# Decay scores as column tiles and dense norms in three parts, in a two-block transformer kernel

## The chip, the cores and the metric

The kernel runs on one core of a Trainium2 chip. The metric is the device time in microseconds (us) from the first to the last instruction of one execution and the little that lies around it; the median over several executions counts.

## What is computed

The reference takes 512 tokens of width 1024 through two blocks, all in float32. The first block has two layers, each with modulated RMS norm, sliding-window attention beside a pooling mixer, and a gated feed-forward part (width 2816). The second has a token mixer of two branches and a mixture of 32 experts. The change touches the norms between the parts of the first block and the first branch of the mixer, HGRN2 with 8 heads in both directions:

```python
x = x + gate_m * rms_norm(mix, g_post_mix[l])
h = rms_norm(x, g_pre_ffn[l]) * (1.0 + scale_f) + shift_f
f = (jax.nn.silu(h @ w_gate[l]) * (h @ w_up[l])) @ w_down[l]
x = x + gate_f * rms_norm(f, g_post_ffn[l])
...
# one direction of HGRN2: S_t = diag(f_t) S_{t-1} + k_t^T v_t, o_t = q_t S_t, k_t = 1 - f_t
decay = jnp.exp(jnp.where(causal, G[:, :, :, None, :] - G[:, :, None, :, :], -jnp.inf))
attn = jnp.einsum('bhtd,bhsd,bhtsd->bhts', qb, kb, decay)
o = jnp.einsum('bhts,bhsv->bhtv', attn, vb) + jnp.einsum('bhtd,bhdv->bhtv', qb * jnp.exp(G), S)
```

So the score of tokens s and t carries, for each of a head's 128 channels, the product of all forget gates f between them.

## The kernel before

**Layout and precision.** Activations lie transposed, channels on partitions and 512 tokens along a row, in eight blocks of 128 channels. Weights and activations are split into a high and a low part (`split_into`, L115: ACT writes the high part, DVE subtracts for the low one), and a product is three matmuls (`mm3`, L154: high by high, high by low, low by high). Weight slabs come by DMA on SP's queue into three `raw` buffers and are split into four `w` buffers (`W1`, L879), one for each 128 output columns. PSUM has four buffers `acc`, three `t` and one `mod`.

**The order of the work.** A planner fixes each engine's order when the kernel is built: of the instructions whose inputs and buffers it reckons ready, the one that stands earliest in the program goes next. On the chip each engine keeps that order and waits where an input is late. Moving a piece of code later therefore lowers its rank; it doesn't move it if nothing else is ready.

**Dense norms.** `out_phase` (L852) computes an output projection in eight blocks m; `slabs[m // 2]` holds the weights. In the last pass (`final`) blocks 0 to 3 are done for 512 tokens, then blocks 4 to 7 for the first 256 tokens and again for the last 256 (`half`). `stats` (L399) sums squares into `acc`. After block 7 of each half, `norms` (L420) is written out: `row_sums` (L344, PE, tile `st`), `rstd` (ACT's square root, DVE's reciprocal), `spread` (L355, PE, tile `rb`), and then for each of eight blocks the update of x and the next H, mostly on DVE. The next projection begins with the first half's tokens (`pj` in L706 for layer 1, `pg` and `pu` at L826 for the feed-forward part), with k in the outer loop over four weight tiles, and the first KE = 3 k steps of the second half after that. There are four such places with `final`: after the mixer and after the feed-forward part of each layer. After the fourth come the decay heads, whose first projection (`pj`) takes 512 tokens at once.

**Decay heads.** `hgrn` (L1155) projects, for each head, q, the two forget gates, the value (every second head) and the output gate. The rest of a head, `hg_head` (L1074), is a generator; `pump` (L449) lets it go one step for every 2.25 units of three matmuls of the next head, so its work stands between the next head's projections. KS holds the keys of both directions (1 - f), QP the queries times decay, TOT the products of f over growing runs of tokens. The scores between tokens of the same pair of runs, of h = 1, 2, 4, ... 64 tokens, are one level each: four matmuls of 128x128 (L1114, float32, two records each in the trace), of which only the entries of that level are wanted; `copy_predicated` (L1118) copies those by a mask into AD. Then `update` (L1084) multiplies KS on DVE (L1086) and QP on POOL (L1088) by the totals (tile `tot`, L1094), and `copies` (L1078) writes X and Y for the next level on ACT. Z (L1098, POOL) gives the scores of a token with itself (L1105). The products across 128-token chunks are `l1` (L1124) and `l2` (L1135). Last, the scores are split (`th` on ACT, `tl` on DVE, L1147 and L1148) and multiplied by the value (tile `po`), and `head_norm` (L1013) normalises the head with one reciprocal of 128x512 (L1026). The retention heads call it too.

Of the kernel before, what the change touches and what calls it, by code (L numbers as in the profile page):

```python
# [10 lines left out]
F32 = mybir.dt.float32  # L11
# [17 lines left out]
KE = 3  # L29
WG = 0  # L30
# [40 lines left out]
class K:  # L71
# [348 lines left out]
    def norms(self, h, F, gg, gs, sh, H):  # L420
# [4 lines left out]
        sums = self.row_sums(self.acc if both else self.acc[:1], h)  # L425
        r = self.small([128, 4], "rs", bufs=4)
# [250 lines left out]
    def layer(self, l, P, v, H, nxt, W=None):  # L677
# [138 lines left out]
        for nk in (6, 8, 8):  # L816
            G = []
            for j in range(k0 // 2, (k0 + nk) // 2):
# [9 lines left out]
                if j == 0:  # L828
                    for h, n in ((0, 8), (1, KE)):
                        for k in range(n):  # L830
                            for b in range(2):
                                self.gemm_cols(Wg, H, 8, b, pgu[b][0], half=h, ks=[k])
                                self.gemm_cols(Wu, H, 8, b, pgu[b][1], half=h, ks=[k])
# [18 lines left out]
    def out_phase(self, slabs, G, nk, F, final, gg, gs=None, sh=None):  # L852

        nc = self.nc
        newF = F or [self.blk("Q", F32, "f") for _ in range(8)]
        order = [(m, None) for m in range(4 if final else 8)]
        if final:
            order += [(m, h) for h in range(2) for m in range(4, 8)]
        pst = {}
        H = None  # L860
        for m, h in order:
            if m not in pst:
                pst[m] = self.ps("po")
            p = pst[m]
            self.gemm_cols(slabs[m // 2], G, nk, m % 2, p, half=h)
            hs = slice(0, 512) if h is None else slice(h * 256, h * 256 + 256)
            if F is None:
                nc.scalar.activation(newF[m][:, hs], p[:, hs], AF.Copy)
            else:
                nc.vector.tensor_tensor(newF[m][:, hs], newF[m][:, hs], p[:, hs], op=OP.add)  # L870
            if final:
                self.stats(newF[m][:, hs], m, hs, gg, gs is not None)
                if m == 7:
                    H = H or self.newH()
                    self.norms(h, newF, gg, gs, sh, H)
        return H or newF

# [14 lines left out]
    def block1(self):  # L892
# [21 lines left out]
        return self.layer(1, P1, v1, H, (None, None))  # L914
# [5 lines left out]
LEVELS = (1, 2, 4, 8, 16, 32, 64)  # L920
# [3 lines left out]
def const_masks():  # L924
    s = np.arange(128)[:, None]
    t = np.arange(128)[None, :]
    m = [(s // (2 * h) == t // (2 * h)) & (s // h != t // h) for h in LEVELS]
# [21 lines left out]
class K2(K):  # L949
    B2 = dict(O=16, M=8)  # L950
    HG = dict(KS=2, QP=2, X=2, Y=2, TA=1, TB=2, TH=2, TL=2, AD=1, q=2, T=2, sg=2)
# [61 lines left out]
    def head_norm(self, po, sg, g, n, O):  # L1013
# [12 lines left out]
        nc.vector.reciprocal(r, r)  # L1026
# [47 lines left out]
    def hg_head(self, j, KS, QP, TOT, q, V, sg, gcol, O):  # L1074
# [9 lines left out]
        def update(h, TOT):  # L1084
# [3 lines left out]
            nc.gpsimd.tensor_tensor(w, w, self.other(TOT, h, seg=1), op=OP.mult)  # L1088
# [7 lines left out]

        Z = self.blk("X", F32, "X")
        nc.gpsimd.tensor_tensor(Z, KS[:, 0:512], KS[:, 512:1024], op=OP.add)  # L1098
# [3 lines left out]
        p = self.ps("lv", tag="t")  # L1102
        for i in range(4):
            c = slice(i * 128, (i + 1) * 128)
            nc.tensor.matmul(p[:, c], lhsT=Z[:, c], rhs=q[:, c], start=True, stop=True)  # L1105
        AD = self.blk("AD", F32, "AD")
        nc.scalar.activation(AD, p, AF.Copy)
        yield
        ADv = AD.rearrange("p (i c) -> p i c", i=4)
        for li, h in enumerate(LEVELS):  # L1110
            p = self.ps("lv", tag="t")
            for i in range(4):
                c = slice(i * 128, (i + 1) * 128)
# [27 lines left out]
        for i in range(4):  # L1141
            th, tl = self.blk("TH", F32R, "th"), self.blk("TL", F32R, "tl")
            a = i // 2
            for dst, src in ((slice(i * 128, (i + 1) * 128), AD[:, i * 128:(i + 1) * 128]),
# [3 lines left out]
                nc.vector.tensor_tensor(tl[:, dst], src, th[:, dst].bitcast(F32), op=OP.subtract)  # L1148
            yield
            vs = slice(i % 2 * 256 + vc.start, i % 2 * 256 + vc.stop)  # L1150
            self.mm3(po, V[0][a][:, vs], V[1][a][:, vs], th, tl, i == 0, i == 3)
        yield
        yield from self.head_norm([po], [sg], [gcol], 128, [O])

    def hgrn(self, H, O, v2):  # L1155
# [5 lines left out]
        for j in range(8):  # L1161
            c0 = 128 * j
            self.drain(1)
            W = self.half_slab(w, O_HQ + c0)
            p = self.gemm_m(H, W, 0)
# [4 lines left out]
            for d, off in enumerate((O_FF, O_FB)):  # L1170
                W = self.half_slab(w, off + c0)
                p = self.gemm_m(H, W, 0)
# [15 lines left out]
            W = self.half_slab(w, O_HG + c0)  # L1188
            p = self.gemm_m(H, W, 0)
# [110 lines left out]
    def mixer(self, H):  # L1300
# [4 lines left out]
        with self.phase("b2", side="right", **self.B2):  # L1305
# [3 lines left out]
            with self.phase("hg", side="right", **self.HG):  # L1309
                self.masks = self.ph.tile([128, 896], U8, name="masks")  # L1310
                r = self.raw()
                nc.scalar.dma_start(r[:, :896], A["msk"])
                nc.gpsimd.tensor_copy(self.masks, r[:, :896])
# [781 lines left out]
```

## Time and profile before

| what | us |
|---|---|
| median of 3 executions | 2533.7 (2531.62 to 2534.28) |
| the profiled execution | 2530.84 |
| its span, first to last instruction | 2529.0 |
| TensorE clock granted over the span | 0.979 of full speed |
| first block, up to the last output projection's end | about 1162 |
| decay heads (HGRN2) and the branch's gates behind them | about 1162 to 1560 |
| retention, branch, mixer output | about 1560 to 2010 |
| experts, weights at some 420 GB/s | about 2010 to 2529 |

The profile is of one execution. PE is the matmul engine, PEld its weight load (beside PE), DVE the vector engine, ACT the scalar engine, POOL the general one, SP the engine whose queue issues most DMAs. Line numbers are those of the kernel before. A row of the timeline has the start, the time and the instruction, with its output and input tiles (out<-in), partitions by elements, and in brackets the idle time of the engine before it and what ended that. PEclk is the share of full clock granted: 1.00 is 2.4 GHz, 0.50 is 1.2 GHz. Matmuls are pipelined: a record lasts longer than the step from one start to the next.

### The profile page before, as it was taken

Reading aid. Unit: us, or ns where it says so; the run is one execution under the profiler, and the core shown is the slowest. Engines: PE = TensorE matmul, PEld = TensorE weight load, DVE = VectorE, ACT = ScalarE, POOL = GpSimd, SP = SyncE. Lnnn points to the kernel's source line nnn. Section 1 sums busy time; section 2 is a strip of 40 time slices with the busy share of each in tenths; the row PEclk is TensorE's granted clock in tenths of the full one; section 3 lists DMA queues with packets and bytes.
Section 4 is the critical chain, followed back from the end, with each engine's and each line's share of the span. In section 5 each row is a group of like instructions: output and inputs, shape, how many; then the busy total and the mean of one; then the engine's idle time right before and its main releaser. Section 6 shows DMA issues by size and latency. Waiting matters only on the chain. (4 is left out here: it accounts for less than half of the span.)

```text
span 2529.0 us, 30517 instructions
## 1 busy us (share of the span) xinstructions
PE 2408.8 (95%) x11804; PEld 1757.0 (69%) x11804; DVE 1372.4 (54%) x2203; ACT 907.3 (36%) x1577; POOL 366.6 (14%) x358
## 2 busy tenths in 40 slices
PE   7999999999899999998999999999999999989996
PEld 3668777778788888887787787887887643433332
DVE  4867566437977233336788786356544444222224
ACT  3654232223664222224555555233332211112111
POOL 1324000005433000002332331010000000000000
PEclk9998999999998999999999999999999999999998
DMA  7531576432212233222121122222223599989995
GB/s 259 186 111 59 200 278 215 155 100 68 64 58 63 88 100 100 84 82 76 59 76 51 42 92 78 97 78 75 90 77 133 199 374 414 423 367 424 423 423 248
DMA packets 221295, 416.60 MB, mean 165 GB/s; under 512 B 11746, under 2 KB 185294, under 8 KB 193500
## 3 DMA queue, kind: packets, MB, share of 16 engines
q1 hardware_dynamic: 214752, 406.07, 44.3%
q0 software_dynamic: 2736, 5.83, 0.6%
q10 hardware_dynamic: 3660, 2.72, 0.4%
q8 instruction: 94, 1.54, 0.2%
q14 instruction: 53, 0.43, 0.0%
HBM read 414.01 MB, written 4.72 MB: 166 GB/s over the span
## 5 line engine op out<-in xcount | busy, mean ns | idle before, releaser
L149 DVE TENSOR_TENSOR w<-raw,w 128x1024 fp32r<-128x1024 f32 (+2 forms) x216 | 263.4, 1221 | 231.1 <-ACT w L148 231.1
L148 ACT ACTIVATE w<-raw 128x1024 fp32r<-128x1024 f32 (+2 forms) x228 | 229.0, 1010 | 375.0 <-PE pu L158 149.1
L156 PE MATMUL pj<-Hh,w 128*128 128x512 f32 (+1 forms) x704 | 280.8, 403 | 5.9 <-ACT Hh L392 3.5
L157 PE MATMUL pj<-Hl,w 128*128 128x512 f32 (+1 forms) x704 | 277.9, 396 | 6.8 <-DVE Hl L395 6.8
L158 PE MATMUL pj<-Hh,w 128*128 128x512 f32 (+1 forms) x704 | 274.0, 390 | 0.0
L1833 PE MATMUL gu<-ew,x 128*64 128x512 f32 (+2 forms) x1024 | 247.1, 599 | 0.0
L158 PE MATMUL po<-Gh,w 128*128 128x512 f32 (+1 forms) x608 | 212.4, 349 | 0.0
L156 PE MATMUL po<-Gh,w 128*128 128x512 f32 (+1 forms) x608 | 211.7, 349 | 0.5 <-ACT Gh L621 0.5
L157 PE MATMUL po<-Gl,w 128*128 128x512 f32 (+1 forms) x608 | 211.2, 347 | 0.0
L156 PE MATMUL pu<-Hh,w 128*128 128x512 f32 (+1 forms) x448 | 171.7, 383 | 0.1
L157 PE MATMUL pu<-Hl,w 128*128 128x512 f32 (+1 forms) x448 | 170.9, 381 | 0.0
L158 PE MATMUL pu<-Hh,w 128*128 128x512 f32 (+1 forms) x448 | 170.8, 382 | 0.0
L1833 PEld LDWEIGHTS gu<-ew,x 128*64 128x64 f32 (+2 forms) x1024 | 75.0, 134 | 136.0 <-issue 121.3
L157 PEld LDWEIGHTS pj<-Hl,w 128*128 128x128 f32 x704 | 135.5, 193 | 42.3 <-DVE Hl L395 9.1
L158 PEld LDWEIGHTS pj<-Hh,w 128*128 128x128 f32 x704 | 134.5, 191 | 35.5 <-issue 7.7
L156 PEld LDWEIGHTS pj<-Hh,w 128*128 128x128 f32 x704 | 134.5, 193 | 34.2 <-ACT Hh L392 4.6
L157 PE MATMUL pg<-Hl,w 128*128 128x512 f32 (+1 forms) x384 | 148.0, 386 | 7.2 <-DVE Hl L395 6.9
L156 PE MATMUL pg<-Hh,w 128*128 128x512 f32 (+1 forms) x384 | 146.8, 382 | 0.0
L158 PE MATMUL pg<-Hh,w 128*128 128x512 f32 (+1 forms) x384 | 146.7, 382 | 0.0
L1889 DVE SCALAR_TENSOR_TENSOR yl<-yp,wsm,yh 128x512 fp32r<-128x512 f32 x30 | 22.5, 751 | 212.0 <-ACT yh L1888 210.5
L1088 POOL TENSOR_TENSOR QP<-QP,tot 128x512 f32<-128x512 f32 x64 | 102.9, 1611 | 219.1 <-ACT Y L1081 171.1
L158 PEld LDWEIGHTS po<-Gh,w 128*128 128x128 f32 x608 | 114.4, 188 | 19.5 <-issue 4.2
(519 smaller groups left out, 4737.5 us busy)
## 6 DMA issues: line engine op xcount, KB each, us to landing
ew<-in_w SPq DMA_DIRECT2D x192, 1024.0 KB
raw<-in_w_in SPq DMA_DIRECT2D x34, 1024.0 KB
raw<-in_ada_w SPq DMA_DIRECT2D x24, 1024.0 KB
raw<-in_w_gate SPq DMA_DIRECT2D x22, 1024.0 KB
raw<-in_w_up SPq DMA_DIRECT2D x22, 1024.0 KB
raw<-in_ada_w SPq DMA_DIRECT2D x40, 512.0 KB
raw<-in_w_in SPq DMA_DIRECT2D x40, 512.0 KB
raw<-in_w_down SPq DMA_DIRECT2D x16, 1024.0 KB
```

What stands on the lines that cost most here:

```text
L148: nc.scalar.activation(hv[:, k], rv[:, k], AF.Copy)
L149: (nc.gpsimd if b in self.low else nc.vector).tensor_tensor(lv[:, k], rv[:, k], hv[:, k].bitcast(F32), op=OP.subtract)
L156: nc.tensor.matmul(out, lhsT=wh, rhs=ah, start=first, stop=False)
L157: nc.tensor.matmul(out, lhsT=wh, rhs=al, start=False, stop=False)
L158: return nc.tensor.matmul(out, lhsT=wl, rhs=ah, start=False, stop=last)
L1088: nc.gpsimd.tensor_tensor(w, w, self.other(TOT, h, seg=1), op=OP.mult)
L1833: self.plast = self.nc.tensor.matmul(out[n * j:n * j + n, :], lhsT=X[k // 4][:, k % 4 * 128 + n * j:k % 4 * 128 + n * j + n], rhs=w, start ...
L1889: v.scalar_tensor_tensor(lo, p, ws, hi.bitcast(F32), op0=OP.mult, op1=OP.subtract)
```

## The change

- *Norms.* `norms` becomes a generator with a stop after the row sums and one at its end, and is only made, not run, after block 7. For the first half it is resumed before block 4 of the second half (row sums) and in the middle of that block (all the rest). For the second half it is resumed in the new `halves`, after k steps 0, 1 (row sums) and 2, 3 (the rest) of the next projection's first half.
- *Five blocks.* With HALVES = 5 blocks 3 to 7 are done by token halves; block 7 takes the PSUM buffer `mod`.
- *Head 0.* The new `first_head` computes the four projections of decay head 0 (not the value) by `halves` at the end of the first block.
- *Levels.* The new `blocks` computes scores only in diagonal blocks, by column tiles: sixteen matmuls of 32 by 32 for Z and for h = 1 to 16, collected in AC (128x4x32) with smaller masks; for h = 32 sixteen of 32 by 32 and for h = 64 eight of 64 by 64 between neighbouring blocks, copied without a mask. ACT copies AC and the two large levels into AD (ten copies).
- *Engines.* QP's update and Z move from POOL to DVE.
- *Score split.* The split of score operand i + 1 stands before the matmuls of operand i.
- *Reciprocal.* `head_norm` takes it in four pieces of 128.

```diff
@@ norms
         sums = self.row_sums(self.acc if both else self.acc[:1], h)
+        yield
         r = self.small([128, 4], "rs", bufs=4)
...
             self.stages(KB, add, lambda m: self.split_into(H[m][0][:, hs], H[m][1][:, hs], self.x[m][:, hs]))
+        yield
@@ layer, projection of layer 1 (the feed-forward part's first projection likewise)
-        for h, n in ((None, 8),) if l == 0 else ((0, 8), (1, KE)):
-            for k in range(n):
+        if l:
+            self.halves(H, [((W, W0)[i // 2], i % 2, pst[i]) for i in range(4)], KE)
+        else:
+            for k in range(8):
                 for i in range(4):
-                    part((W, W0)[i // 2], i % 2, pst[i], half=h, ks=[k])
+                    part((W, W0)[i // 2], i % 2, pst[i], ks=[k])
@@ out_phase
-        order = [(m, None) for m in range(4 if final else 8)]
-        if final:
-            order += [(m, h) for h in range(2) for m in range(4, 8)]
+        first = 8 - HALVES if final else 8
+        order = [(m, None) for m in range(first)]
+        order += [(m, h) for h in range(2) for m in range(first, 8)]
...
-                pst[m] = self.ps("po")
+                pst[m] = self.ps("po", tag="mod" if final and m == 7 else "acc")
             p = pst[m]
-            self.gemm_cols(slabs[m // 2], G, nk, m % 2, p, half=h)
+            if h == 1 and m == first + 1:
+                self.resume()
+                self.gemm_cols(slabs[m // 2], G, nk, m % 2, p, half=h, ks=range(nk // 2))
+                self.resume()
+                self.gemm_cols(slabs[m // 2], G, nk, m % 2, p, half=h, ks=range(nk // 2, nk))
+            else:
+                self.gemm_cols(slabs[m // 2], G, nk, m % 2, p, half=h)
...
-                    self.norms(h, newF, gg, gs, sh, H)
+                    self.norm = self.norms(h, newF, gg, gs, sh, H)
...
+    def halves(self, H, out, n):
+        for h, ks in ((0, 8), (1, n)):
+            for k in range(ks):
+                for W, b, p in out:
+                    self.gemm_cols(W, H, 8, b, p, half=h, ks=[k])
+                if h == 0 and k in (1, 3):
+                    self.resume()
@@ block1, hgrn
-        return self.layer(1, P1, v1, H, (None, None))
+        H = self.layer(1, P1, v1, H, (None, None))
+        self.first_head(H)
+        return H
...
+    def first_head(self, H):
+        W = [self.half_slab(self.A["w_in_2"], o) for o in (O_HQ, O_FF, O_FB, O_HG)]
+        self.head0 = [self.ps("pj") for _ in W]
+        self.halves(H, [(w, 0, p) for w, p in zip(W, self.head0)], KE)
+        for w, p in zip(W, self.head0):
+            self.gemm_cols(w, H, KB, 0, p, half=1, ks=range(KE, KB))
@@ head_norm
-        nc.vector.reciprocal(r, r)
+        for i in range(4):
+            nc.vector.reciprocal(r[:, i * 128:(i + 1) * 128], r[:, i * 128:(i + 1) * 128])
@@ hg_head
-            nc.gpsimd.tensor_tensor(w, w, self.other(TOT, h, seg=1), op=OP.mult)
+            nc.vector.tensor_tensor(w, w, self.other(TOT, h, seg=1), op=OP.mult)
...
+        def blocks(X, Y, w, flip):
+            p = self.ps("lv", tag="t")
+            for i in range(4):
+                for b in range(128 // w):
+                    l, r = (slice(i * 128 + c * w, i * 128 + c * w + w) for c in (b, b ^ flip))
+                    nc.tensor.matmul(p[b * w:b * w + w, i * w:i * w + w], lhsT=X[:, l], rhs=Y[:, r],
+                                     start=True, stop=True, tile_position=(0, b * w))
+            return p[:, :4 * w].rearrange("p (i c) -> p i c", i=4)
...
-        for li, h in enumerate(LEVELS):
-            p = self.ps("lv", tag="t")
-            for i in range(4):
-                c = slice(i * 128, (i + 1) * 128)
-                nc.tensor.matmul(p[:, c], lhsT=X[:, c], rhs=Y[:, c], start=True, stop=True)
+        for li, h in enumerate(SMALL):
+            p = blocks(X, Y, 32, 0)
+            TOT = update(h, TOT)
+            X, Y = copies(2 * h)
+            nc.vector.copy_predicated(AC, self.masks[:, li * 32:li * 32 + 32][:, None, :].to_broadcast([128, 4, 32]), p)
+            yield
+        for b in range(4):
+            rows = slice(b * 32, b * 32 + 32)
+            nc.scalar.activation(ADv[rows, :, rows], AC[rows], AF.Copy)
+        for h in LARGE:
+            p = blocks(X, Y, h, 1)
             TOT = update(h, TOT)
             if h < 64:
                 X, Y = copies(2 * h)
-            nc.vector.copy_predicated(ADv, self.masks[:, li * 128:(li + 1) * 128][:, None, :].to_broadcast([128, 4, 128]),
-                                      p.rearrange("p (i c) -> p i c", i=4))
+            for b in range(128 // h):
+                nc.scalar.activation(ADv[b * h:b * h + h, :, (b ^ 1) * h:(b ^ 1) * h + h], p[b * h:b * h + h], AF.Copy)
             yield
...
+        t = parts(0)
+        for i in range(4):
+            nxt = parts(i + 1) if i < 3 else None
             yield
...
-            self.mm3(po, V[0][a][:, vs], V[1][a][:, vs], th, tl, i == 0, i == 3)
+            self.mm3(po, V[0][i // 2][:, vs], V[1][i // 2][:, vs], *t, i == 0, i == 3)
+            t = nxt
```

## Rows read from the trace of the kernel before

**Rows 1.** The page's totals by engine: busy us (share of the span) x instructions.

```profile
PE 2408.8 (95%) x11804; PEld 1757.0 (69%) x11804; DVE 1372.4 (54%) x2203; ACT 907.3 (36%) x1577; POOL 366.6 (14%) x358
```

**Rows 2.** Stretches, columns as in the first line: four dense norms, then the decay heads.

```profile
core 0: us, PE busy (x) PEld busy (x) DVE busy (x) ACT busy (x) POOL busy (x), PEclk, DMA share, GB/s
199.00:247.00 48.00, 42.33 (x299) 40.00 (x298) 35.66 (x78) 21.38 (x43) 22.12 (x29) 0.86 0.11 34
597.00:645.00 48.00, 43.45 (x315) 40.64 (x314) 37.80 (x80) 20.45 (x42) 26.23 (x32) 0.93 0.14 45
762.00:810.00 48.00, 41.70 (x294) 39.40 (x293) 34.81 (x76) 21.20 (x42) 19.43 (x24) 0.86 0.14 45
1150.00:1186.00 36.00, 28.25 (x159) 24.36 (x158) 26.87 (x63) 17.81 (x34) 13.07 (x15) 0.86 0.24 74
1195.00:1552.00 357.00, 342.10 (x1890) 289.47 (x1889) 284.59 (x389) 191.96 (x332) 118.96 (x72) 0.98 0.22 67
```

**Rows 3.** First dense norm: DVE's low-part splits of weights in time, then a stretch.

```profile
205.97 1.23 DVE L149 TENSOR_TENSOR w<-raw,w 128x1024 fp32r<-128x1024 f32 x1
...
223.56 1.21 DVE L149 TENSOR_TENSOR w<-raw,w 128x1024 fp32r<-128x1024 f32 x1
...
213.90:222.90 9.00, 6.46 (x32) 5.21 (x31) 8.53 (x21) 4.96 (x11) 5.01 (x7) 0.72 0.00 0
```

**Rows 4.** Timeline of PE at the norm ahead of the decay heads.

```profile
1167.24 1.02 PE L352 MATMUL st<-ones,acc 128*128 128x2 f32 x4 [4.70 <-DVE acc L408]
...
1172.67 1.65 PE L156 MATMUL pj<-Hh,w 128*128 128x512 f32 x3 [2.40 <-ACT Hh L121]
```

**Rows 5.** What PE waited for in the decay heads: us in total, times, longest.

```profile
PE po L157 <- DVE tl L1148: 9.5, 6, 2.6
PE l L1135 <- POOL QP L1088: 2.8, 5, 1.8
PE po L156 <- ACT th L1147: 1.1, 3, 0.4
```

**Rows 6.** Timeline of one place in the decay heads, POOL, DVE and PE.

```profile
1326.53 3.87 POOL L1088 TENSOR_TENSOR QP<-QP,tot 128x512 f32<-128x512 f32 x2
...
1328.67 2.53 DVE L1094 TENSOR_TENSOR tot<-tot 128x768 f32<-128x768 f32 x1
...
1332.26 1.87 DVE L1094 TENSOR_TENSOR tot<-tot 128x384 f32<-128x384 f32 x1
...
1334.52 0.79 PE L157 MATMUL po<-tl,vh 128*128 128x512 f32 x1 [2.57 <-DVE tl L1148]
```

**Rows 7.** Decay heads by line and shape: busy us, mean ns, idle before.

```profile
L1086 DVE TENSOR_TENSOR KS<-KS,tot 128x512 f32<-128x512 f32 x64 | 74.9, 1171 | 17.1 <-ACT X L1080 15.8 <-POOL X L1098 1.2
...
L1181 DVE TENSOR_TENSOR QP<-q,tot 128x512 f32<-128x512 f32 x14 | 9.5, 682 | 0.0
...
L1118 DVE COPY_PREDICATED AD<-masks,lv 128x512 f32<-128x512 uint8 x56 | 40.9, 731 | 0.4
...
L1088 POOL TENSOR_TENSOR QP<-QP,tot 128x512 f32<-128x512 f32 x64 | 102.9, 1611 | 219.1 <-ACT Y L1081 171.1 <-DVE tot L1094 32.4 <-PE l L1124 9.0
...
L1080 ACT ACTIVATE X<-KS 128x512 f32<-128x512 f32 x55 | 36.7, 667 | 16.8 <-DVE KS L1086 14.1 <-PE lv L1114 2.6
```

**Rows 8.** Timeline of PE: one level's score matmuls (x8 merged) and the next matmul.

```profile
1261.70 1.05 PE L1114 MATMUL lv<-Y,X 128*128 128x128 f32 x8
1262.51 0.48 PE L156 MATMUL pj<-Hh,w 128*128 128x512 f32 x1
```

**Rows 9.** Timeline of PE: the modulation's column tiles (x8 merged) between full matmuls.

```profile
353.01 0.40 PE L157 MATMUL pu<-Hl,w 128*128 128x512 f32 x1
353.24 0.40 PE L158 MATMUL pu<-Hh,w 128*128 128x512 f32 x1
353.57 1.06 PE L286 MATMUL mod<-moda,ones 128*32 128x512 f32 x8
354.56 0.50 PE L156 MATMUL pg<-Hh,w 128*128 128x512 f32 x1
```

**Rows 10.** Sixteen 40-column records: ns min/median/max, first and last start.

```profile
L1383 PE MATMUL sc<-wr,lnv x16: 202/202/202, 1952.3 to 1952.8; 128*1 128x40 f32 x16
```

More of the change, by code (lines that the diff above doesn't have):

```diff
@@ L29 @@
 KE = 3
+HALVES = 5
 WG = 0
@@ L828, in layer @@
                 if j == 0:
[L829 to L833, printed above, removed]
+                    self.halves(H, [(w, b, pgu[b][i]) for b in range(2) for i, w in enumerate((Wg, Wu))], KE)
                 for b in range(2):
@@ L874, in out_phase, with resume @@
                     H = H or self.newH()
-                    self.norms(h, newF, gg, gs, sh, H)
+                    self.norm = self.norms(h, newF, gg, gs, sh, H)
         return H or newF
+    def resume(self):
+        next(self.norm)
+    def halves(self, H, out, n):
[5 more added lines that the diff above has]
+                    self.resume()
     B1 = dict(G=16, Q=12, U=4, TH=4, TL=4, TA=2, TB=1)
@@ L919 @@
 ALPHA = 2.0 ** 0.25
-LEVELS = (1, 2, 4, 8, 16, 32, 64)
+SMALL, LARGE = (1, 2, 4, 8, 16), (32, 64)
 O_HQ, O_FF, O_FB, O_HI, O_HG, O_RQ, O_RK, O_RV, O_RG, O_GA, O_GB = [1024 * i for i in range(11)]
 def const_masks():
-    s = np.arange(128)[:, None]
-    t = np.arange(128)[None, :]
-    m = [(s // (2 * h) == t // (2 * h)) & (s // h != t // h) for h in LEVELS]
+    s = np.arange(128)[:, None] % 32
+    t = np.arange(32)[None, :]
+    m = [(s // (2 * h) == t // (2 * h)) & (s // h != t // h) for h in SMALL]
     return np.ascontiguousarray(np.concatenate(m, axis=1).astype(np.float32))
@@ L1101, in hg_head @@
         yield
-        p = self.ps("lv", tag="t")
-        for i in range(4):
-            c = slice(i * 128, (i + 1) * 128)
-            nc.tensor.matmul(p[:, c], lhsT=Z[:, c], rhs=q[:, c], start=True, stop=True)
+        p = blocks(Z, q, 32, 0)
         AD = self.blk("AD", F32, "AD")
-        nc.scalar.activation(AD, p, AF.Copy)
+        ADv = AD.rearrange("p (i c) -> p i c", i=4)
+        AC = self.blk("AC", F32, "AC", (128, 128)).rearrange("p (i c) -> p i c", i=4)
+        nc.scalar.activation(AC, p, AF.Copy)
         yield
-        ADv = AD.rearrange("p (i c) -> p i c", i=4)
-        for li, h in enumerate(LEVELS):
-            p = self.ps("lv", tag="t")
-            for i in range(4):
-                c = slice(i * 128, (i + 1) * 128)
-                nc.tensor.matmul(p[:, c], lhsT=X[:, c], rhs=Y[:, c], start=True, stop=True)
+        for li, h in enumerate(SMALL):
[9 more added lines that the diff above has]
+            p = blocks(X, Y, h, 1)
             TOT = update(h, TOT)
@@ L1140, in hg_head, with parts @@
         po = self.ps("po")
-        for i in range(4):
+        def parts(i):
             th, tl = self.blk("TH", F32R, "th"), self.blk("TL", F32R, "tl")
@@ L1163, in hgrn @@
             self.drain(1)
-            W = self.half_slab(w, O_HQ + c0)
-            p = self.gemm_m(H, W, 0)
+            cols = lambda o: self.head0.pop(0) if j == 0 else self.gemm_m(H, self.half_slab(w, o + c0), 0)
+            p = cols(O_HQ)
             q = self.blk("q", F32, "q")
@@ L1309, in mixer @@
             with self.phase("hg", side="right", **self.HG):
-                self.masks = self.ph.tile([128, 896], U8, name="masks")
+                self.masks = self.ph.tile([128, 160], U8, name="masks")
                 r = self.raw()
-                nc.scalar.dma_start(r[:, :896], A["msk"])
-                nc.gpsimd.tensor_copy(self.masks, r[:, :896])
+                nc.scalar.dma_start(r[:, :160], A["msk"])
+                nc.gpsimd.tensor_copy(self.masks, r[:, :160])
                 self.hgrn(H, O, v2)
```

13 lines of the change are left out of this document (6 added, 7 removed).

## The prediction

> **What bounds the kernel now.** I read the page's totals first [rows 1]: PE is busy 2408.8 of 2529.0 us, DVE 54%, ACT 36%, POOL 14%. So time is won only where PE stands still, runs at its lower clock level, or does needless work. The stretches [rows 2] say where that is, in the parts that the change touches. I reckon the loss of a stretch as its length less PE's busy time, plus busy time times (1 - granted clock), since at 0.50 (the 1.2 GHz level) a matmul takes twice as long as at 1.00 (2.4 GHz). Of the four places where a dense norm follows a projection, the first three lose 5.7+5.9, 4.6+3.0 and 6.3+5.8 us, together 31; the fourth, on the way to the decay heads, loses 7.8+4.0 = 11.7 of 36 us. The decay heads, 357 us, lose 14.9 us to waits and 342.1 x 0.02 = 7 us to the clock, 22 in all; PE is busy there 96%, DVE 80%.
>
> Why PE loses it differs. At the first norm only the first of the next projection's four weight low halves is written before the norm of the first token half claims DVE: one at 205.97, the next at 223.56 [rows 3]; from 213.9 to 222.9 DVE is busy 8.5 of 9.0 us while PE is underfed at clock 0.72. The limit there is DVE's work, not where PE's sums stand. At the fourth norm PE has nothing else: it waits 4.70 us for the row sums and 2.40 us for the first split H [rows 4], because head 0's matmuls take 512 tokens at once. In the decay heads PE waits 9.5 us for the low parts of the score operand (tl), 2.8 for QP from POOL, 1.1 for the high parts [rows 5]. The cause of the first shows in one place [rows 6]: while POOL works on QP (from 1326.53, 3.87 us for two), DVE's 128x768 product takes 2.53 us and the 128x384 one 1.87, PE's wait for tl ends at 1334.52 after 2.57 us, and DVE is in order.
>
> **The change part by part.** *Norms in three parts, three dense places.* The row sums, the spread and the adds move behind half blocks or k steps. DVE's work for them is the same, and it is the limit. The fifth half block gives about one half block's statistics to the time before the norm; but five half blocks hold five weight tiles and the pool has four, so block 7's first half waits until block 3's second half is done and its weights are split. I reckon its end 1.5 to 2 us later (ACT's split, then DVE's 1.2 [rows 3], partly beside PE's next block). The weight split of the next projection may by that come ahead of the norm, which feeds PE a second weight. I take 0; ends -10 (a third of the 31 lost) and +6 (2 us at each of the three).
>
> *Norm to head 0.* The four head-0 projections now run by token halves, so that PE has the first half's H (being written while PE still ran the last output block) to work on during the second half's norm. Two of four weights come late as above; I leave 3.2 of the 11.7 us: **-8.5**, ends -11 and -4. Head 0 holds four weight slots and the main PSUM buffers; the evacuations queue behind it, and PE has the value projection meanwhile. Its four loads on SP's queue move ahead of the value load and, for the raw buffers, of the mask load on ACT's queue, which is needed only when head 1 is projected; with the DMA engines 24% busy there [rows 2] I put that at 0.
>
> *Decay levels.* A head has eight score groups (Z and seven levels). One before takes eight records of 128 columns, from 1261.70 to the next matmul at 1262.51 [rows 8]: 0.81 us. After: sixteen matmuls of 32x32, 32 records, for Z and six levels, and eight matmuls of 64x64, sixteen records, for the last. The nearest rows are the modulation's column tiles [rows 9]: eight records of 512 columns in tiles of 32 take 353.57 to 354.56, 0.99 us. Alone, a record of four times 128 columns would take 0.40 to 0.45, eight in turn over 3.2; so four tiles run side by side, and two sets of 0.45 leave 0.1 for the way back. The way in costs 0.33 against 0.23 between matmuls before it, 0.1 more. How long a stream of 32 columns takes: sixteen records of 40 columns start within 0.5 us [rows 10], 0.033 apiece, so 0.029. The group then takes 8 sets x 0.029 + 0.2 = 0.43, 0.38 less, x 56 groups = 21; the 64-wide one 8 x 0.056 + 0.2 = 0.65, 0.16 less x 8 = 1. The other end is tiles one after another: 32 x 0.029 + 0.2 = 1.13, +18, and +2 for the 64-wide. The column tiles with their own streams [rows 9] are the nearest rows, only shorter here: I take **-20**, ends -23 and +20.
>
> *Updates on DVE alone, in the decay heads.* POOL loses 64 QP products (mean 1.61 us) and eight sums [rows 7]. A clean 128x512 product on DVE takes 0.68 (q by f); the KS products, which share time with POOL, take 1.17 on average [rows 7]. So DVE gives back 64 x 0.49 = 31 and takes (64 + 8) x 0.68 = 49; masked copies fall from 56 x 0.73 = 41 to 40 of a quarter of the elements, each between 0.18 and 0.73, so 7 to 29. DVE goes from 284.6 us to between 269 and 291, in a stretch that should last about 323: not the bound, but 83 to 90% busy. Preparing the next score operand one step ahead gives tl and th a further step of slack. Ten more small ACT copies a head lie beside PE, ACT being busy 54% [rows 2]; that cover goes if the copies fall on the last steps, where AD is due only three steps on. Of the 22 us of waits and clock I take **-14**, ends -20 (the named waits and their clock dips gone) and 0 (new waits for QP, now behind KS on DVE).
>
> *Small parts.* Reciprocals in four pieces, smaller masks, half-width matmuls for a fifth block and head 0: +0.5; the pieces lie on DVE beside PE.
>
> Sum: 0 - 8.5 - 20 - 14 + 0.5 = -42. From the profiled execution's 2530.84 (2529.0 span and 1.8 around it) to 2488.8; the median of the runs is 2.9 above that execution, so **2492 us**. The later parts, bound by PE and then by the expert weights' transfers, which start once the mixer ends, move forward whole.
>
> **The rivals.** *A, tiles in turn.* If tiles with so short a stream don't overlap, the levels cost +20 in place of -20: 2532, within the noise. For it: no row has 32-column streams in tiles. Against: the 0.99 us for eight long ones [rows 9]. Chance 0.13.
>
> *B, slower: the level chain is in series.* One level needs KS and QP on DVE (2 x 0.69), then X and Y copies on ACT (2 x 0.67) [rows 7], 2.7 us, and 3.3 with the mask copy and the product of the totals; PE has per step 2.25 x 3 matmuls of 0.23 and a group of 0.43, 2.0 us. If the planner puts the groups earlier than the chip has the copies, PE waits 0.7 to 1.3 us at 64 groups; at 1.0 it is +64, so 2556. It ends slower from 42/64 = 0.65 us a group on. Against: the chain with POOL was longer, and of PE's three long waits none is at a level's group (l is the product across chunks) [rows 5]. Chance 0.08.
>
> *C, all three dense norms freed.* If PE's waits there come from where the sums stand rather than from DVE, the 31 us go too: 2461. For it: at the fourth norm the wait is for the sums. Against: the weight splits [rows 3]. Chance 0.10.
>
> *D, a floor under short streams.* If a 32-column record costs as much as one of 60 columns, 0.05 a set, the group takes 0.60, saving 0.21 x 56 + 1 = 13 in place of 20: 2499. The rows of 40 columns at 0.033 [rows 10] speak against it. The Trainium skill says in TensorEngine Tiling (Array Packing), section Instruction Overhead, that a matmul carries some 60 cycles, so that one column takes as long as sixty, and advises against tiling a dimension already small; by this the sum would be -35 and not -42, and those sixteen records don't bear it out for the rate, though nothing here shows it for tiles. Chance 0.12.
>
> **How the numbers follow.** Forecast 0.57, A 0.13, B 0.08, C 0.10, D 0.12. Faster or slower is counted from 0.2% (5 us), about what a measurement of this kernel tells from no change. Faster: forecast, C, D and 0.02 of A, 0.81; within: 0.09 of A; slower: B and 0.02 of A, 0.10. The forecast's own range is 2474 (every gain but the dense norms at its better end, and 6 us of those) to 2513 (waits stay, tiles at D's price). To hold 8 in 10 it must reach A on the upper side: 2472 to 2534; left out are B and C, 0.18.
>
> **What the changed profile would show.** The score groups: from the first record to the next full matmul 0.43 us if right, 0.6 with a floor, 1.1 in turn. POOL idle in the decay heads, KS at 0.69, DVE 83 to 90% busy, PE's tl wait of 9.5 us gone, the clock 1.00 but for a dip or two. At the fourth norm a PE wait of 1 to 3 us in place of 7. At the three dense norms the same loss, about 10 us each, with block 7's first half behind block 3's second. Wrong I'd be most if PE waits at the level groups for X or Y, or if the dense norms' clock dips are gone.

## The result and the profile after

| kernel | runs | median us | lowest to highest | ratio to before (95% interval) |
|---|---|---|---|---|
| before | 4 | 2532.66 | 2529.40 to 2534.28 | |
| after | 4 | 2491.68 | 2489.78 to 2499.45 | 0.9845 (0.9834 to 0.9857) |
| after, measured again | 5 | 2493.35 | 2488.35 to 2500.20 | 0.9853 (0.9835 to 0.9871) |

The forecast was 2492, with 2472 to 2534 as its range. The profiled execution of after is the slowest of its four, 2499.45, or 7.8 above their median; the experiments show where that excess lies.

The page's totals of after, beside [rows 1]: PE has 20 us less to do, and POOL 120 us less.

```profile
PE 2388.4 (96%) x13404; PEld 1728.6 (69%) x13404; DVE 1343.3 (54%) x2304; ACT 929.5 (37%) x1667; POOL 246.2 (10%) x292
```

The last two stretches of [rows 2] in after, with the decay heads up to their new end, about 1520:

```profile
1150.00:1186.00 36.00, 34.26 (x283) 33.49 (x282) 22.44 (x46) 13.71 (x27) 7.74 (x10) 1.00 0.25 76
...
1195.00:1520.00 325.00, 320.42 (x3333) 251.73 (x3332) 262.51 (x488) 221.48 (x424) 0.00 (x0) 0.99 0.25 77
```

The first three norms lie 4.5, 11 and 15 us later in this execution than before: their row sums start at 205.3, 608.3 and 777.5 us, before at 200.8, 597.3 and 762.7. The same stretches of time would cover other work, so each of these starts 2 us ahead of the first row sums and ends 60 us behind them, first for before, then for after:

```profile
198.80:260.80 62.00, 56.33 (x376) 52.10 (x375) 45.73 (x90) 28.65 (x51) 22.32 (x29) 0.89 0.21 69
595.30:657.30 62.00, 54.67 (x372) 49.29 (x371) 51.12 (x95) 29.78 (x55) 32.66 (x36) 0.94 0.18 54
760.70:822.70 62.00, 55.70 (x374) 51.64 (x373) 43.32 (x85) 28.64 (x51) 20.22 (x26) 0.89 0.21 64
...
203.30:265.30 62.00, 52.96 (x338) 48.17 (x337) 46.96 (x90) 28.14 (x53) 24.63 (x30) 0.89 0.22 72
606.30:668.30 62.00, 53.59 (x342) 48.50 (x341) 50.86 (x96) 29.53 (x57) 34.22 (x37) 0.89 0.20 61
775.50:837.50 62.00, 54.79 (x369) 49.39 (x368) 48.59 (x90) 30.42 (x55) 21.88 (x26) 0.97 0.23 73
```

Losses counted as in the prediction: before, these stretches lose 11.9, 10.6 and 12.4 us, 35 together; in after 14.9, 14.3 and 8.9, or 38 together. In the second profile of after, at the same places, they lose 11.9, 12.8 and 8.8, or 34. The fourth norm, which lies some 10 us later here, loses 1.7 in place of 11.7 (and from 1160 to 1196, where PE is busy 34.26 us at 1.00, 1.7 again). In the decay heads PE is busy 99% of a stretch that is 32 us shorter, DVE 81%, POOL not at all. In this execution the last output projection of the first block ends at 1172.8 us, against 1162.5 before; the first level group starts at 1215.1 against 1213.5; the last level record starts at 1511.3 against 1544.8. So about 10 us were lost up to the last projection, 8.7 won from there to the level groups, and 35 won in the decay heads.

PE's waits in after from 1195 to 1560, beside [rows 5] (us in total, times, longest):

```profile
PE lv L1127 <- ACT Y L1105: 2.9, 4, 2.1
PE l L1173 <- DVE QP L1112: 1.7, 1, 1.7
```

The 9.5 us for tl are gone. Of what is left, waits of 2.1 and 1.7 us end at 1510.7 and 1515.4, in the last head, which has no projections of a next head beside it.

PE's timeline in after: a 32-wide level group (against [rows 8]), a 64-wide one, and the norm ahead of the decay heads (against [rows 4]):

```profile
1214.80 0.40 PE L159 MATMUL pj<-Hh,w 128*128 128x512 f32 x1
1215.13 0.46 PE L1127 MATMUL lv<-q,X 128*32 128x32 f32 x32
1215.52 0.50 PE L157 MATMUL pj<-Hh,w 128*128 128x512 f32 x1
...
1230.12 0.39 PE L159 MATMUL pj<-Hh,w 128*128 128x512 f32 x1
1230.43 0.69 PE L1127 MATMUL lv<-Y,X 128*64 128x64 f32 x16
1231.05 0.50 PE L157 MATMUL pj<-Hh,w 128*128 128x512 f32 x1
...
1175.66 0.36 PE L157 MATMUL pj<-Hh,w 128*128 128x256 f32 x1 [1.37 <-DVE f L877]
...
1177.39 0.50 PE L353 MATMUL st<-ones,acc 128*128 128x2 f32 x4
...
1178.72 0.39 PE L159 MATMUL pj<-Hh,w 128*128 128x256 f32 x1 [0.36 <-DVE w L123]
```

The group takes 0.39 us from its first record to the next full matmul, 0.81 before, and the step into it 0.33 against 0.23. That saves 0.81 + 0.23 - 0.39 - 0.33 = 0.32 us at 56 groups. The 64-wide one takes 0.62 and saves 0.11 at eight: together 19 us.

At the fourth norm the row sums come without a wait and PE stands 1.37 + 0.36 us, where it stood 4.70 + 2.40.

DVE's groups in after, 1195 to 1520, against [rows 7]:

```profile
L1110 DVE TENSOR_TENSOR KS<-KS,tot 128x512 f32<-128x512 f32 x64 | 47.7, 746 | 16.3 <-ACT X L1104 13.4 <-PE l L1162 1.9
L1112 DVE TENSOR_TENSOR QP<-QP,tot 128x512 f32<-128x512 f32 x64 | 47.5, 743 | 5.3 <-ACT Y L1105 5.1
...
L1146 DVE COPY_PREDICATED AC<-masks,lv 128x128 f32<-128x128 uint8 x40 | 11.9, 297 | 2.4 <-PE lv L1127 2.0
```

KS fell from a mean of 1.17 to 0.75 us, so that KS and QP on DVE together (95 us) cost only 20 more than KS alone before, and the masked copies fell by 29.

### The profile page after: what moved, and what is told of

Same layout as the page of the kernel before. It is cut to its first block, busy times and chain, and to the rows that moved or that the text cites. A ratio compares the mean times of both kernels' runs of the same rounds, so it can differ in the third digit from the quotient of the medians.

```text
span 2497.7 us, 33723 instructions
## 1 busy us (share of the span) xinstructions
PE 2388.4 (96%) x13404; PEld 1728.6 (69%) x13404; DVE 1343.3 (54%) x2304; ACT 929.5 (37%) x1667; POOL 246.2 (10%) x292
## 5 line engine op out<-in xcount | busy, mean ns | idle before, releaser
L157 PE MATMUL pj<-Hh,w 128*128 128x512 f32 (+1 forms) x736 | 284.4, 391 | 7.2 <-ACT Hh L393 5.8
L159 PE MATMUL pj<-Hh,w 128*128 128x512 f32 (+1 forms) x736 | 279.3, 381 | 0.4 <-DVE w L123 0.4
L157 PE MATMUL po<-Gh,w 128*128 128x256 f32 (+1 forms) x640 | 218.9, 343 | 0.5 <-ACT Gh L624 0.5
L159 PE MATMUL po<-Gh,w 128*128 128x256 f32 (+1 forms) x640 | 218.3, 342 | 0.0
L158 PE MATMUL po<-Gl,w 128*128 128x256 f32 (+1 forms) x640 | 217.3, 341 | 0.0
L158 PEld LDWEIGHTS pj<-Hl,w 128*128 128x128 f32 x736 | 140.5, 191 | 37.3 <-DVE Hl L396 7.2
L159 PEld LDWEIGHTS pj<-Hh,w 128*128 128x128 f32 x736 | 140.3, 191 | 35.2 <-issue 7.9
L157 PEld LDWEIGHTS pj<-Hh,w 128*128 128x128 f32 x736 | 138.4, 190 | 37.1 <-ACT Hh L393 7.4
L157 PEld LDWEIGHTS po<-Gh,w 128*128 128x128 f32 x640 | 121.8, 190 | 17.9 <-issue 1.7
L159 PEld LDWEIGHTS po<-Gh,w 128*128 128x128 f32 x640 | 121.9, 190 | 17.4 <-issue 3.4
```

What stands on the lines that cost most here:

```text
L157: nc.tensor.matmul(out, lhsT=wh, rhs=ah, start=first, stop=False)
L158: nc.tensor.matmul(out, lhsT=wh, rhs=al, start=False, stop=False)
L159: return nc.tensor.matmul(out, lhsT=wl, rhs=ah, start=False, stop=last)
```

## The experiments: the decay heads

**Decay heads alone.** The dense norms and head 0 go back to the old form:

```diff
-HALVES = 5
+HALVES = 4
...
-                    self.norm = self.norms(h, newF, gg, gs, sh, H)
+                    for _ in self.norms(h, newF, gg, gs, sh, H):
+                        pass
...
-        self.first_head(H)
+        self.head0 = []
...
```

> Decay heads as after; the four dense norms and head 0 as before (four half blocks, norms in one piece, head 0 over 512 tokens). Theory 1 (the prediction's terms: decay heads -34, norm to head 0 -8.5, three dense norms 0): 2532.7 - 34 = about 2499, 7 us above after. Theory 2 (the profiled execution of after: the three dense norms cost it +10 and head 0 gives back 8.7): undoing both leaves 2491.7 + 8.7 - 10 = about 2490, no slower than after.

Measured: 2496.73 (2494.58 to 2500.25), ratio 0.9860 (0.9845 to 0.9875), which is 35.0 below the 2531.7 of before beside it. Theory 2 falls. The decay heads bring 35, and all the rest of the change brings 3 to 5.

**The old level scores, the rest as after.** Four full matmuls a group, wide masked copies into AD:

```diff
-            p = blocks(X, Y, 32, 0)
+            p = self.ps("lv", tag="t")
+            for i in range(4):
+                c = slice(i * 128, (i + 1) * 128)
+                nc.tensor.matmul(p[:, c], lhsT=X[:, c], rhs=Y[:, c], start=True, stop=True)
...
```

> After with the old level scores: Z and seven levels as four full 128x128 matmuls each and the wide masked copies into AD; QP and Z still on DVE, the split still one step ahead. Theory 1 (column tiles save what their records show: way in and group 0.715 us against 1.040 for 56 groups, 0.933 against 1.040 for 8, so 19 us): 2491.7 + 19 = about 2511. Theory 2 (the groups lay beside other limits and the gain of the decay heads came from DVE): 2492 to 2497. Theory 3 (DVE, with the wide masked copies 29 us busier, makes PE wait again): 2517 or more.

Measured: 2512.52 (2508.61 to 2518.12), ratio 0.9928 (0.9916 to 0.9940): 19 to 21 above after, as the records say. Theory 1 holds. DVE is 298 us busy there, and PE waits no more than in after. Its windows row for 1195 to 1552 (columns as in [rows 2]) and the group in its timeline:

```profile
1195.00:1552.00 357.00, 352.36 (x1985) 300.28 (x1984) 298.38 (x524) 208.63 (x357) 0.00 (x0) 1.00 0.23 71
```

```profile
1215.18 0.40 PE L159 MATMUL pj<-Hh,w 128*128 128x512 f32 x1
1215.41 1.05 PE L1137 MATMUL lv<-Y,X 128*128 128x128 f32 x8
1216.22 0.48 PE L157 MATMUL pj<-Hh,w 128*128 128x512 f32 x1
```

**QP and Z back on POOL, the rest as after.**

```diff
-            nc.vector.tensor_tensor(w, w, self.other(TOT, h, seg=1), op=OP.mult)
+            nc.gpsimd.tensor_tensor(w, w, self.other(TOT, h, seg=1), op=OP.mult)
...
-        nc.vector.tensor_tensor(Z, KS[:, 0:512], KS[:, 512:1024], op=OP.add)
+        nc.gpsimd.tensor_tensor(Z, KS[:, 0:512], KS[:, 512:1024], op=OP.add)
```

> After with QP's update and Z back on POOL; column tiles and the split one step ahead stay. Theory 1 (POOL beside DVE stretches DVE's products and brings PE's waits back; this is most of the 14 us for waits and clock): KS mean back from 0.75 to about 1.1 us, 2499 to 2506. Theory 2 (one step of slack for the score split is enough to hide a stretched DVE): 2490 to 2494. Theory 3 (POOL's help is worth more than the stretch, since DVE falls from 81% busy): under 2490.

Measured: 2528.58 (2524.62 to 2533.92, 11 runs), ratio 0.9986 (0.9977 to 0.9995): 35 to 37 above after, outside all three expectations. The direction is theory 1's, the size two and a half to five times it. The waits of PE in this kernel, 1195 to 1560, and its windows row (columns as in [rows 2]):

```profile
PE po L158 <- DVE tl L1187: 13.8, 7, 3.7
PE lv L1127 <- ACT X L1104: 6.5, 4, 1.8
PE lv L1127 <- ACT Y L1105: 4.5, 4, 3.2
PE l L1162 <- DVE tot L1118: 3.3, 3, 1.1
PE l L1173 <- POOL QP L1112: 1.7, 1, 1.7
PE l L1173 <- DVE KS L1110: 1.2, 3, 0.4
...
1195.00:1552.00 357.00, 325.14 (x3330) 254.25 (x3329) 271.82 (x413) 220.70 (x421) 112.53 (x72) 0.97 0.22 66
```

The waits sum to 31 us, against 15 before. In the stretch of the windows row PE stands 31.9 us and loses 9.8 to the clock, 42 together, against 22 before: 20 more, which is what the tiles save of PE's own work. So PE now waits for the products of DVE and POOL, also at the level groups (11 us for ACT's X and Y), where it hardly waited before. ACT's copies Y stand 31.0 us for POOL's QP here and stood 38.4 before, against 3.3 for DVE's QP in after: the chain through POOL was as slow before. That PE's longer groups left it time then is how I read these waits. The level part, from the first level record to the last, tells how the two halves of the change stand to each other:

| kernel | level scores | QP and Z | first to last level record, us |
|---|---|---|---|
| before | full | POOL | 331.3 |
| QP and Z back on POOL | column tiles | POOL | 330.5 |
| old level scores | full | DVE | 312.6 |
| after | column tiles | DVE | 296.2 |

Column tiles with POOL beside them bring nothing; DVE alone brings 19; with DVE the tiles bring 16 more, and the wait of 2.1 us at the last head's level is most of what they lack of their 19.

How POOL does it stands in the timeline of this kernel, DVE, POOL and PE, at one place (the same as [rows 6] before):

```profile
1329.87 2.93 DVE L1110 TENSOR_TENSOR KS<-KS,tot 128x512 f32<-128x512 f32 x1 [1.18 <-POOL X L1132]
...
1333.71 1.20 DVE L123 TENSOR_TENSOR w<-raw,w 128x1024 fp32r<-128x1024 f32 x1
1334.84 1.87 DVE L1118 TENSOR_TENSOR tot<-tot 128x384 f32<-128x384 f32 x1
...
1329.80 2.00 POOL L1112 TENSOR_TENSOR QP<-QP,tot 128x512 f32<-128x512 f32 x1
1333.93 2.37 POOL L1112 TENSOR_TENSOR QP<-QP,tot 128x512 f32<-128x512 f32 x1 [2.13 <-DVE tot L1118]
...
1337.10 0.80 PE L158 MATMUL po<-tl,vh 128*128 128x512 f32 x1 [3.75 <-DVE tl L1187]
```

KS takes 0.69 us at 1322.67, where POOL is at rest, and 2.93 here, where POOL's QP began 0.07 us ahead of it and ran 2.00: about the sum of the two. DVE's weight split, begun before the second QP, takes its usual 1.20, and then QP takes 2.37. The next product on DVE, tot, begins while QP runs, and takes 1.87 where it takes 0.54 in after. PE stands 3.75 us for the low part queued behind it. Some of the delay is POOL's own: the one QP that no DVE instruction overlaps takes 1.06 us, where DVE needs 0.69 for KS. No run parts that from the sharing.

**The split without its step ahead.**

```diff
-        t = parts(0)
         for i in range(4):
-            nxt = parts(i + 1) if i < 3 else None
+            t = parts(i)
             yield
...
-            t = nxt
```

> After with the score split of operand i directly before its matmuls, as before the change; QP and Z stay on DVE. Theory 1 (the waits for tl came from POOL's stretching of DVE, which is gone): 2490 to 2494, waits for tl and th under 3 us. Theory 2 (the step of slack is what hides them): about 2500, PE waits for tl or th 8 us or more in the decay heads.

Measured: 2497.25 (2494.08 to 2502.06), ratio 0.9865 (0.9851 to 0.9879), between the two. Its waits decide, since they are the same as in after, with none for tl or th:

```profile
PE lv L1127 <- ACT Y L1105: 2.9, 4, 2.1
PE l L1173 <- DVE QP L1112: 2.4, 1, 2.4
```

The level part takes 296.1 us, as in after, and from the end of the last output projection to the end of the program it has 1325.2 us, after 1324.9. So its 4 to 5 us lie in the first block, which it shares with after: its last projection ended at 1171.3. In the decay heads the step ahead is worth nothing.

**Column tiles in turn.** Only the order of the same matmuls changes:

```diff
-            for i in range(4):
-                for b in range(128 // w):
+            for b in range(128 // w):
+                for i in range(4):
```

> After with the two loops of the level scores exchanged: all four chunks of one column tile follow each other, then the next tile, so neighbours in the order share a tile. Same matmuls, same results. Theory 1 (tiles run side by side only when neighbours in the order lie in different tiles; eight records in turn per tile at 0.0315 us): group 32 x 0.0315 + 0.13 = 1.1 in place of 0.39, the 64-wide 1.1 in place of 0.62, 56 x 0.7 + 8 x 0.5 = +43, about 2535. Theory 2 (each tile queues on its own and the order among them doesn't matter): group 0.4, 2490 to 2494.

Measured: 2519.68 (2519.27 to 2526.83), ratio 0.9961 (0.9948 to 0.9974): 26 to 28 above after, and 7 above the kernel with full matmuls for the scores. Theory 2 falls; theory 1 is right in kind and too large:

```profile
1208.20 0.40 PE L159 MATMUL pj<-Hh,w 128*128 128x512 f32 x1
1208.53 0.90 PE L1127 MATMUL lv<-q,X 128*32 128x32 f32 x32
1209.36 0.50 PE L157 MATMUL pj<-Hh,w 128*128 128x512 f32 x1
```

The group takes 0.83 in place of 0.39, the 64-wide 0.90 in place of 0.62: 56 x 0.44 + 8 x 0.28 = 27 us, the whole difference. By the starts of the records, those of one tile follow each other at 0.032 us, and only where the order passes from one tile to the next do the two overlap, so the group stays under the 1.1 of rival A. In after four records of four tiles start within 0.02 us, and the next four 0.032 after them.

## The experiments: norms and head 0

**Four half blocks, norms in three parts:**

```diff
-HALVES = 5
+HALVES = 4
```

> After with four half blocks in place of five, norms still in three parts. Theory 1 (five half blocks hold five weight tiles where the pool has four; block 7's first half waits, and the row sums come at 205.3 us instead of 200.8): each dense norm ends 1.5 to 2 us earlier, 2491.7 - 5 = about 2486. Theory 2 (DVE's work limits the dense norms, wherever the sums stand): 2490 to 2493. Theory 3 (the fifth half block gives cover that PE needs): 2494 or more.

**Five half blocks, norms in one piece** (the calls of `resume` in `out_phase` and `halves` go too):

```diff
-                    self.norm = self.norms(h, newF, gg, gs, sh, H)
+                    for _ in self.norms(h, newF, gg, gs, sh, H):
+                        pass
```

> After with five half blocks, but each norm written in one piece as before (head 0 by token halves). Theory 1 (DVE's work is the limit, so the places of row sums, spread and adds are worth nothing): 2490 to 2493. Theory 2 (the pieces let PE go on where it waited for sums): 2491.7 + 4 x 1.5 = about 2498. Theory 3 (the pieces themselves cost the +10 that the profile of after shows at the dense norms): about 2484.

**Four half blocks, norms in one piece** (both edits above together, head 0 still by token halves), measured twice:

> After with four half blocks and norms in one piece, head 0 still by token halves (that part of the change alone left in). Theory 1 (prediction: the dense part is worth 0): 2490 to 2493. Theory 2 (it costs 5 by the weight tiles alone): about 2486. Theory 3 (the +10 that the profile shows): about 2482.

> The kernel with old norms and head 0 by halves once more, unchanged (first 2489.3, runs from 2486.4 to 2490.0), since after itself gave 2491.7 and 2493.4 with runs from 2488 to 2500. Theory 1 (the dense part of the change costs 2 to 4 us, and makes the time unsteady): 2488 to 2490 again, runs within 4 us. Theory 2 (dense part 0, the difference is chance): 2491 to 2494, runs spread over 8 us or more.

**After once more**, unchanged:

> The kernel after, unchanged, once more beside the others, to compare them on one chip. Theory 1 (five half blocks with four weight tiles cost the first block some 7 us: in five kernels with this dense part the last projection ended at 1166 to 1173 us, in three with four half blocks at 1164): 2494 to 2498, 6 us above the kernel with old norms and head 0 by halves (2489.3). Theory 2 (the first median stands): 2490 to 2493.

**Three half blocks**, norms in one piece:

```diff
-HALVES = 4
+HALVES = 3
```

> Norms in one piece and head 0 by token halves (as the kernel with old norms), with three half blocks in place of four. Theory 1 (the count of weight tiles decides: with three the fourth tile can hold a weight of the next projection before the norm claims DVE): no later row sums cost, a gain of 2 to 4, 2485 to 2487. Theory 2 (the norm's cover decides: three half blocks are 8.4 us of PE work for 9 us of DVE): each dense norm 2 us longer, 2495 or more.

**Two of four weight low halves on POOL**, four half blocks, norms in one piece:

```diff
-                self.low = LF if j in LG else ()
+                self.low = (1,) if j == 0 else LF if j in LG else ()
...
```

> The kernel with old norms and head 0 by halves (2489.3), with the low halves of two of the four weights behind norms 1 and 3 written on POOL in place of DVE. Theory 1 (DVE's work is the limit of these norms, the weight splits queue on it): the last projection's end 2 to 5 us earlier, 2484 to 2487. Theory 2 (POOL's 2.7 us for one such split, or the sharing with DVE, takes it back): 2488 to 2492.

| half blocks | norms | median us | lowest to highest | ratio (95% interval) |
|---|---|---|---|---|
| 5 | three parts (after) | 2491.68, 2493.35 | 2488.35 to 2500.20 | 0.9845, 0.9853 |
| 5 | one piece | 2496.88 | 2496.20 to 2498.78 | 0.9865 (0.9850 to 0.9880) |
| 4 | three parts | 2490.27 | 2487.98 to 2493.44 | 0.9839 (0.9826 to 0.9852) |
| 4 | one piece | 2489.25 | 2486.44 to 2489.99 | 0.9828 (0.9814 to 0.9841) |
| 4 | one piece, again | 2487.31 | 2484.84 to 2491.09 | 0.9817 (0.9803 to 0.9830) |
| 3 | one piece | 2491.72 | 2488.33 to 2493.93 | 0.9841 (0.9827 to 0.9854) |
| 4 | one piece, POOL splits | 2490.03 | 2488.63 to 2491.19 | 0.9833 (0.9820 to 0.9847) |

What follows.

- *Head 0* by token halves: 2496.73 without it (decay heads alone), 2489.25 and 2487.31 with it, so -7.5 to -9.4.
- *Five half blocks* in one piece cost 7.6 to 9.6 over four, and their intervals lie apart. Row sums of the first norm start at 203.8 us instead of 201.3 in the two profiles; in all seven profiles with five half blocks they start between 202.3 and 205.3, in the five with four between 200.2 and 201.7. In the order that the planner wrote for after, block 7's first half starts behind all of block 3's second half and ten matmuls of block 4's.
- *Three parts* come out 3.5 to 5 lower with five half blocks, but the intervals overlap, and the last projection ends at 1169.8 us in one piece and between 1164.3 and 1173.1 in the six profiles in three parts: a gain isn't shown. With four half blocks they bring nothing.

By the expectations, theory 2 holds with four half blocks in three parts (2490.27, within its 2490 to 2493), and with five in one piece theory 2 is nearest (2496.88 for 2498). Old norms came out at 2489.25, between theories 1 and 2, and then at 2487.31, a little beyond theory 1's 2488, with runs spread over 6 us. After once more fell on the edge of its two theories. By the pooled medians, 2491.7 of nine runs of after and 2488.3 of ten with old norms, the dense part of the change costs 3.4 us; by the ratios 0.0027, or 7.

It also makes the time unsteady: after's runs spread over 12 us, those with old norms over 6. In the second profile of after the last output projection ended at 1164.3, in the first at 1172.8, and the rest of the program took 1324.7 and 1324.9. So the 7.8 us by which the first profiled execution lies above its median are made in the first block, in runs of one and the same program. They go with the clock: over the span 0.982 was granted in the first profile and 0.985 in the second, and of all nine runs the slowest (2500.20) had 0.980 and the fastest (2488.35) 0.987.

The windows rows of 199 to 260 (columns as in [rows 2]) show why placing is worth so little. First with four half blocks in three parts, then in one piece:

```profile
199.00:260.00 61.00, 52.72 (x358) 47.88 (x357) 45.16 (x89) 27.82 (x50) 22.79 (x28) 0.94 0.22 70
```

```profile
199.00:260.00 61.00, 54.88 (x371) 50.89 (x370) 44.18 (x88) 28.55 (x51) 22.67 (x29) 0.89 0.20 61
```

In parts PE stands 8.3 us and loses 3.2 to the clock; in one piece it stands 6.1 and loses 6.0. Half of the clock's loss goes and waits take its place: 11.5 us are lost against 12.2.

Three half blocks missed both theories: neither the tiles in the weight pool nor the cover of the second halves decides alone, and four has the lowest median of the three counts. Moving weight splits to POOL came out as theory 2 has it, no faster. PE waits for POOL's split in place of DVE's H, and later for a split on DVE; its timeline, PE then POOL:

```profile
221.83 0.58 PE L159 MATMUL pu<-Hh,w 128*128 128x256 f32 x1 [2.49 <-POOL w L150]
...
252.73 0.79 PE L159 MATMUL pg<-Hh,w 128*128 128x512 f32 x1 [3.48 <-DVE w L150]
...
219.25 2.52 POOL L150 TENSOR_TENSOR w<-raw,w 128x1024 fp32r<-128x1024 f32 x1
```

No run has a fifth weight buffer beside five half blocks, which would show the pool's part by itself. That the missing buffer is the cause of the 7.6 to 9.6 us therefore rests on the order and on the count of half blocks and isn't shown. The version with old norms, new decay heads and head 0 by halves is below both kernels: 0.9828 and 0.9817 of before, against after's 0.9845 and 0.9853.

## Why the prediction was right, and where it was not

The forecast's total held to within 1 us of the first median and 2 of the second. That close a hit is partly luck: one term was 3 to 7 us off, and the medians of after themselves lie 2 us apart. The terms, one by one:

- *Norm to head 0*, -8.5: measured -7.5 to -9.4. The wait for row sums went as said, and one late weight of 0.36 us is left where I had reckoned two.
- *Column tiles*, -20: the records give -19, the runs -19 to -21. The group alone was 0.39, not 0.43, since 0.43 held the way in; with the way in it is 0.39 + 0.10 = 0.49. A set of four took 0.0315 where I had 0.029, and the two ways together 0.23 where I had 0.2. D's 0.05 a set didn't come.
- *Waits and clock*, -14 of 22: in after 4.6 us of waits and 3.2 to the clock are left, so 14 went, as said; counted in the level part with the old scores, DVE alone brings 18.7. DVE's 262.5 us lie under my 269 to 291, since I had left out what else POOL stretched: without it the products of the totals (`tot`) take 10 us less and the splits `tl` 7. Masked copies came near my lower end (11.9 of 7 to 29 us), and KS fell to 0.75, not to 0.68. Half of the reason given for the term fell: I leaned on the split one step ahead as well, and that is worth nothing.
- *Three dense norms*, 0 with ends -10 and +6: the dense part as a whole measured +3 to +7, at the wrong end. The two steps that I named both came true. Block 7's first half runs behind block 3's second. A second weight is split early: two low halves are written by 214.9 us and the next projection starts on two weights at 218.62, where before the second low half came at 223.56 [rows 3]. What I missed is what follows: PE soon waits 2.87 us for a low half of the next four weights, a wait that before doesn't have up to 262 us. From DVE's timeline, then PE's:

```profile
211.31 1.57 DVE L150 TENSOR_TENSOR w<-raw,w 128x1024 fp32r<-128x1024 f32 x1 [0.32 <-ACT w L149]
213.68 1.21 DVE L150 TENSOR_TENSOR w<-raw,w 128x1024 fp32r<-128x1024 f32 x1
...
257.27 0.50 PE L159 MATMUL pg<-Hh,w 128*128 128x512 f32 x1 [2.87 <-DVE w L150]
```

The one thing wrong in kind is hidden by the sum: I added the tiles' -20 and the engines' -14 as if each stood alone. With POOL the tiles are worth 0.8 us of level part, not 20, because the products of DVE and POOL then end last; the two together bring 35.1, more than 0.8 and 18.7 apart. In part that is rival B's mechanism, a chain off PE that sets the end at the level groups (11 of the 31 us of waits; 13.8 are for `tl`). It shows as soon as POOL is in it, and I had argued against B from POOL's chain being the longer one. In after B doesn't decide: 4.6 us of waits, nearly all in the last head.

Rival A shows two thirds of its price in the run with the tiles in turn (27 us of 40), but its condition isn't met, since the change's own order alternates the tiles. C fell: some dips of the clock went, which I had named as what would make me most wrong. At the third norm (0.97 for 0.89) 3.5 us went with them; at the second, PE stands longer and 2 to 4 us were lost in both profiles, and the three together gain nothing (35 before, 38 and 34 in after). That the limit there is DVE's work agrees with the placings that moved the sums and not the time, yet the run that took splits off DVE won nothing, so what sets the pace of a dense norm is not settled.

## What to carry to other kernels

Two savings on different engines of one loop need not add up: take each away by itself, from the finished kernel, and see what the loop costs; here the tiles were worth 16 to 21 us or nothing, by who did the products beside them. Small matmuls in column tiles paid here with neighbours in the order in different tiles; in another order the same matmuls cost 27 us more, and 7 more than the full ones that they replaced. A stall that can be moved and not shortened, like the dense norms here, comes back as a wait where the clock dip was; a profile of the clock alone would have called that a gain.

## What the runs showed of the hardware

- Four column tiles side by side cost what one does: a set of four 32-column records takes 0.0315 us, and one record in turn 0.032. Going into the tiles costs 0.10 us over a common step, coming out about as much.
- Records of 32, 64 and 128 columns follow each other at 0.032, 0.058 and 0.112 us, but in each the weights have as many columns as the stream. The row sums keep 128 columns of weights and stream two columns, and eleven of their steps take 1.25 us, 0.11 each, as long as with 128. So these runs don't give the price of a short stream by itself. The Trainium skill, TensorEngine Tiling (Array Packing), section Instruction Overhead, has one column take as long as sixty and advises against tiling a small dimension. In the row sums two columns do take as long as many more; at 32 columns in tiles, the tiling paid (0.39 us a group for 0.81). The row sums in after:

```profile
205.32 1.50 PE L353 MATMUL st<-ones,acc 128*128 128x2 f32 x12 [0.56 <-DVE acc L409]
```

- DVE and POOL didn't slow each other in part, they took turns: 2.93 us for a product of 0.69 beside one of 2.00, while a weight split that had begun first kept its 1.20. In the decay heads of that kernel 26 KS products begin while POOL is in an instruction, and 21 of them end 0.54 to 0.55 us behind it; of the 18 that begin first, 17 keep their 0.68 to 0.69. The Trainium skill says in SBUF — State Buffer, section "SBUF: two separate sides", that the port which the two share is locked for a whole instruction by whichever starts first; the rows above agree.
